# Turning row tiles one by one into shared banks at the start of a hybrid decoder block

## The chip, the cores and the metric

The kernel runs on one core of one Trainium2 chip. The metric is the device time of one execution in microseconds (us); less is better. Engines are named as the profile names them: PE is TensorE's matmul, PEld its weight load, DVE is VectorE, ACT is ScalarE, POOL is GpSimd and SP is SyncE, whose queue issues the loads and stores. "Bank" always means a PSUM bank; the kernel uses eight (a pool of six, `bank`, and one of two, `bank2`), each as a tile of 128 partitions by 512 float32.

## The reference

The block takes `x` of 512 rows by 1024 columns in float32, with one layer:

```python
h = rmsnorm(x, norm1_g)
z = h @ w_in + b_in                      # 1024 -> 6656 columns
z_glu, z_rx, z_rg, z_ga, z_gb = split(z) # two token mixers and their gates
y_a = conformer_convolution(z_glu)       # gated, 31 taps, layer norm, product
y_b = rg_lru(z_rx, z_rg)                 # 4 taps, gates per head, recurrence, product
m = sigmoid(z_ga) * y_a + sigmoid(z_gb) * y_b
x = x + m @ w_mix_out
h = rmsnorm(x, norm2_g)
x = x + (silu(h @ w1) * (h @ w3)) @ w2
return rmsnorm(x, norm_f_g)
```

Only the first two lines matter here: the first norm, and the beginning of the product with `w_in`.

## The kernel before

`x` lies in four row tiles of 128 rows, each in two halves of 512 columns (`xt[t][h]`). PE contracts over the partitions, so the normed rows have to be turned: channels must lie on the partitions. There are eight groups of 128 channels, in the text "channels 0 to 7", and each has a tile pair `h1{c}h` and `h1{c}l` of 128 channels by 512 rows. Every operand of a product is held as a high part (a copy in PE's `float32r`) and a low part (what the copy left off), and a product is three: high with high, low of the rows with high of the weights, high of the rows with low of the weights (`mm3`, L469).

The opening works on two pairs of row tiles, 0 and 1, then 2 and 3; a pair gives one half (256 columns) of every `h1` tile.

- `norm1_rows(t)` (L530) norms one row tile. ACT sums the squares of each half (L494, L500) and takes the root (L501); DVE adds the epsilon (L495), takes the reciprocal (L502) and scales both halves in place (L534).
- `rows_turned(0, n_first)` (L458) turns the first parameter rows, among them the gain `norm1_g`, on PE and copies them to `par` on DVE (L463).
- `turn_half` (L511) takes channel after channel: two transposes on PE, one from each row tile of the pair, into a tile of its own (L518); then ACT makes the high part, scaled by the gain (L521), and DVE the low part from the same tile and the high part (L522).
- A weight chunk is one column block of `w_in`, 512 KB. `emit_chunk` (L143) takes the next one in a fixed list: it issues the load on SP (L152), casts the high part on ACT and subtracts for the low part (`split_to`, L123, with rows L125 and L121), on POOL for the chunks of `w_in`. `emit_to(n)` goes on until n chunks are emitted. Loads go into four rotating buffers.
- `early_mm(i, hf)` (L541) is one of four early products, with the first four chunks, on half `hf` of the rows: 24 products of 256 columns. For the first half the eight products with the weights' low part stand last (`lo_last`).

Inside `tc.manual_schedule` (L550) PE, ACT, DVE and SP issue in the order in which the code is written; POOL's order, and everything behind the block, comes from a planner. Each engine runs its own list in order, and waits on semaphores for the others. The library that puts in those semaphores sees to it that no two engines use one bank at the same time, readers among themselves included. Loads on SP use eight semaphores in rotation: a load waits until the eighth load before it has landed.

Of the kernel before, what the change touches and what calls it, by code (L numbers as in the profile page):

```python
# [8 lines left out]
F32 = mybir.dt.float32  # L9
F32R = mybir.dt.float32r  # L10
AF = mybir.ActivationFunctionType
ALU = mybir.AluOpType

P = 128
# [12 lines left out]
ND = D // P  # L27
# [61 lines left out]
def tile_block(ctx, tc, a, out):  # L89
    nc = tc.nc  # L90
# [14 lines left out]
    def pairt(name, dtype=F32R):  # L105

        return longt(f"{name}h", dtype), longt(f"{name}l", dtype)

    def bank(name):
        return psum.tile([P, T], F32, tag="mm", name=name)  # L110

    def bank2(name):
        return psum2.tile([P, T], F32, tag="cv", name=name)

    vec, act, pe, pool_e = nc.vector, nc.scalar, nc.tensor, nc.gpsimd


    newest = {}
# [4 lines left out]
    def split_to(h, l, full, eng, copy=act.copy):  # L123

        copy(h, full)  # L125
        last = sub(eng, l, full, h.bitcast(F32))
        if eng is pool_e:
            newest["sub"] = last.ins
        return h, l
# [6 lines left out]
    chunks = []  # L136
    held = {}
    emitted = [0]

    def wchunk(key, src, kt, cols, where="hl", lo=pool_e, after=None):  # L140
        chunks.append((key, src, kt, cols, where, lo, after))

    def emit_chunk():  # L143
        key, src, kt, cols, where, lo, after = chunks[emitted[0]]
        emitted[0] += 1
        n = kt * cols
        raw = raws.tile([P, 1024], F32, tag="raw", name=f"raw_{key}")
        rv = raw[:, :n]
        if callable(src):
            src(raw)  # L150
        else:
            newest["load"] = newest["any"] = nc.sync.dma_start(rv.rearrange("p (k n) -> p k n", k=kt), src).ins  # L152
        if where == "hl":
            hl = hls.tile([P, 2, 1024], F32R, tag="hl", name=f"hl_{key}")
            h, l = split_to(hl[:, 0, :n], hl[:, 1, :n], rv, lo)
            if after:
                after(rv, h)
            held[key] = (h.rearrange("p (k n) -> p k n", k=kt), l.rearrange("p (k n) -> p k n", k=kt))
        else:
            held[key] = [  # L160
                split_to(longt(f"{key}h{i}", F32R), longt(f"{key}l{i}", F32R), rv[:, i * T : (i + 1) * T], lo)
                for i in range(2)
            ]

    def emit_to(n):
        while emitted[0] < min(len(chunks), n):
            emit_chunk()
# [6 lines left out]
    w_in = a["w_in"][0].rearrange("(k p) n -> p k n", p=P)  # L174

    def w_in_chunk(m):
        wchunk(f"in{m}", w_in[:, :, m * P : (m + 1) * P], ND, P)

    GLU, RX, RG, GA, GB = 0, 16, 26, 36, 44
    pieces = gate_pieces()  # L180
# [32 lines left out]
    for kind, j in ORDER:  # L213
        if kind == "g":
            gate_chunk(j)
        elif kind == "u":
            w_in_chunk(GLU + j)
            w_in_chunk(GLU + 8 + j)
        elif kind != "r":
            w_in_chunk({"rx": RX, "rg": RG, "gb": GB, "ga": GA}[kind] + j)  # L220
# [187 lines left out]
    n_first = ROWS[0][1] + ROWS[1][1]  # L408
    par = consts.tile([P, n_rows], F32, name="par")
    row_at = lambda c: (0, c) if c < n_first else (1 + (c - n_first) // P, (c - n_first) % P)  # L410
    at, col, parts = 0, {}, []
    for name, n in ROWS:
        col[name] = at
        src = a[name]
        src = src.rearrange("l k (c p) -> (l k c) p", p=P) if len(src.shape) == 3 else src.rearrange("l (c p) -> (l c) p", p=P)
        done = 0
        while done < n:
            m = min(n - done, P - row_at(at + done)[1])
# [5 lines left out]
    def load_rows(i):  # L424
        lo, m, src = parts[i]
        b, r = row_at(lo)
        nc.sync.dma_start(rowt[b][r : r + m, :P], src)  # L427

    x_nat = a["x"].rearrange("b (t p) d -> p (b t) d", p=P)
    xt = [[longt(f"x{t}{h}") for h in range(2)] for t in range(NT)]  # L430

    def load_x(t):
        for h in range(2):
            nc.sync.dma_start(xt[t][h], x_nat[:, t, h * T : (h + 1) * T])  # L434
# [5 lines left out]
    ident = consts.tile([P, P], F32, name="ident")  # L440
# [17 lines left out]
    def rows_turned(c0, c1):  # L458
        pt = bank2(f"par_ps{c0}")
        for c in range(c0, c1, P):  # L460
            m = min(P, c1 - c)
            pe.transpose(pt[:, c - c0 : c - c0 + m], rowt[row_at(c)[0]][:m, :P], ident[:m, :m])
        vec.tensor_copy(par[:, c0:c1], pt[:, : c1 - c0])  # L463

    def pc(name, i):
        return par[:, col[name] + i : col[name] + i + 1]


    def mm3(ps, ws, xs, lo_last=False):  # L469


        n = 3 * len(ws)
        i = 0
        three = [((wh, xh), (wh, xl), (wl, xh)) for (wh, wl), (xh, xl) in zip(ws, xs)]
        if lo_last:
            three = [q[:2] for q in three] + [q[2:] for q in three]
        for l, r in (q for qs in three for q in qs):
            pe.matmul(ps, l, r, start=i == 0, stop=i == n - 1)  # L478
            i += 1

    def w_tiles(key, kt, ahead=AHEAD):
        h, l = weights(key, ahead)
        return [(h[:, k, :], l[:, k, :]) for k in range(kt)]
# [21 lines left out]
    def rstd_of(halves, junk, between=None):  # L505
        begun = rstd_begin(halves[0], junk[0])
        if between:
            between()
        return rstd_end(begun, halves[1], junk[1])

    def turn_half(name, rows, gname, dest, hf, bk, some=range(ND)):  # L511

        cs = slice(hf * 256, hf * 256 + 256)
        for c in some:
            ps = bk[c % len(bk)](f"{name}{hf}{c}")
            for t in range(2):
                src = rows[2 * hf + t][c // 4][:, (c % 4) * P : (c % 4 + 1) * P]
                pe.transpose(ps[:, t * P : (t + 1) * P], src, ident)  # L518
            g = pc(gname, c)
            h, l = (v[:, cs] for v in dest[c])  # L520
            act.activation(h, ps[:, :256], AF.Copy, scale=g)  # L521
            last = vec.scalar_tensor_tensor(out=l, in0=ps[:, :256], scalar=g, in1=h.bitcast(F32), op0=ALU.mult, op1=ALU.subtract)  # L522
        return last.ins

    def parts_of(pair_tiles, cs=slice(0, T)):
        return [(h[:, cs], l[:, cs]) for h, l in pair_tiles]

    h1p = [pairt(f"h1{c}") for c in range(ND)]

    def norm1_rows(t):  # L530
        junk = [shortt(f"n1j{t}{h}") for h in range(2)]
        r = rstd_of(xt[t], junk)
        for h in range(2):
            vec.tensor_scalar(out=xt[t][h], in0=xt[t][h], scalar1=r, scalar2=None, op0=ALU.mult)  # L534

    HALVES = [slice(0, 256), slice(256, 512)]
    EARLY = 2
# [3 lines left out]
    def early_mm(i, hf):  # L541
        m = EARLY_IN[i]
        if hf == 0:
            early.append((m, w_tiles(f"in{m}", ND, 0), bank(f"z{m}")))
        _, ws, ps = early[i]
        mm3(ps[:, HALVES[hf]], ws, parts_of(h1p, HALVES[hf]), lo_last=hf == 0)


    ET = mybir.EngineType
    with tc.manual_schedule(engines={ET.PE, ET.Activation, ET.DVE, ET.SP}):  # L550
        norm1_rows(0)
        norm1_rows(1)
        rows_turned(0, n_first)
        emit_to(1)
        turn_half("tx", xt, "norm1_g", h1p, 0, [bank, bank, bank, bank2])
        emit_to(2)
        load_x(2)
        load_x(3)
        norm1_rows(2)
        norm1_rows(3)  # L560
        emit_to(3)
        for i in range(len(parts)):
            if i not in first:
                load_rows(i)
        early_mm(0, 0)
        early_mm(1, 0)
        turn_half("tx", xt, "norm1_g", h1p, 1, [bank2, bank, bank])
        emit_to(4)
        early_mm(2, 0)
        early_mm(3, 0)  # L570
        rows_turned(n_first, n_rows)
        for i in range(4):
            early_mm(i, 1)
    h1 = parts_of(h1p)


# [252 lines left out]
    for j in range(8):  # L829
        ws = w_tiles(f"lo{j}_0", 5) + w_tiles(f"lo{j}_1", 5)  # L830
        ps = bank(f"yb{j}")
# [113 lines left out]
    for n, j in enumerate(mixq.order()):  # L945
        ws = w_tiles(f"co{j}", ND)
        ps = bank(f"ya{j}")
# [17 lines left out]
    xs = []  # L965
# [75 lines left out]
    for hf in range(2):  # L1041
        if hf:
            turned = turn_half("th", xs, "norm2_g", h2p, 1, [bank2])
        for i in range(EARLY):
            for w_, p_ in zip(wf[i], pf[i]):
                mm3(p_[:, HALVES[hf]], w_, parts_of(h2p, HALVES[hf]))
# [189 lines left out]
```

## Time and profile before

| | before |
|---|---|
| median of three runs | 808.01 us (807.91 to 810.77) |
| the profiled execution | 808.5 us, its span 806.6 us |
| PE busy in the span | 795.6 us (99%) |
| DVE, ACT, POOL busy | 660.2, 455.4, 254.3 us |
| mean granted clock of PE | 0.996 |

The span is what the profile covers, and the time of the execution holds some 1.9 us around it. In a timeline row the first number is the start from the span's beginning in us, the second the duration, then the engine, the line of the code, the operation, the tile written and the tiles read. A note in brackets gives the time for which the engine was idle before the row, and what it waited for. `x2` means that the row merges two instructions. In a table by stretches a row gives the busy time of each engine in that stretch, then the clock that was granted to PE (1.00 is full), the share of the DMA engines and GB/s.

### The profile page before, as it was taken

How to read it: one execution, taken by the hardware profiler on the slowest of the kernel's cores; microseconds unless marked ns; L12 is line 12 of the kernel's file. 1: busy time of each engine (PE TensorE's matmuls, PEld its weight loads, DVE VectorE, ACT ScalarE, POOL GpSimd, SP SyncE). 2: the span in 40 equal slices, each digit the busy share in tenths (PEclk: the TensorE clock that was granted, in tenths of full speed). 3: DMA queues.
4: the chain of work that ended last, by engine and by line, in shares of the span. 5: the costliest groups of instructions: out<-in, count | busy, mean ns of one | idle time of the engine just before them, and what ended most of it. 6: DMA issues, size and time to landing. Idle time of an engine off the chain costs nothing.

```text
span 806.6 us, 11905 instructions
## 1 busy us (share of the span) xinstructions
PE 795.6 (99%) x4182; PEld 687.4 (85%) x4182; DVE 660.2 (82%) x1054; ACT 455.4 (56%) x643; POOL 254.3 (32%) x204
## 2 busy tenths in 40 slices
PE   8999999999999999999999999999999999999996
PEld 7988888888888888888888898999999888888885
DVE  4699899998999998786798869888887954688456
ACT  7546687776589655653336454455555432476443
POOL 3575768766777684231310042000000000000000
PEclk9999999999999999999999999999999999999999
DMA  7746476666667743578978537698889885586552
GB/s 215 191 123 172 134 200 184 181 200 186 192 185 211 228 142 108 190 228 273 298 263 271 152 94 232 195 303 263 262 260 282 241 259 183 163 268 203 177 169 105
DMA packets 207952, 165.02 MB, mean 205 GB/s; under 512 B 13096, under 2 KB 183508, under 8 KB 207892
## 3 DMA queue, kind: packets, MB, share of 16 engines
q1 hardware_dynamic: 207891, 164.26, 67.0%
q8 instruction: 33, 0.54, 0.3%
q14 instruction: 28, 0.22, 0.1%
HBM read 130.80 MB, written 30.41 MB: 200 GB/s over the span
## 4 chain that ended last, share of the span: by engine, by line
PE 96%; DMA 1%; SPq 1%; DVE 0%; POOL 0%; ACT 0%; issue 0%
PE z L478 34%; PE fr L1086 15%; PE f L478 14%; PE or L892 13%; PE yb L478 7%; PE ya L478 5%; PE mxr L892 5%; PE g L764 3%; DMA raw_in<-in_w_in_dram 1%; SPq L434 1%; PE th L518 0%; SPq L427 0%; POOL hl_in L121 0%; DVE of L1159 0%; ACT hl_in L125 0%
## 5 line engine op out<-in xcount | busy, mean ns | idle before, releaser
L637 DVE SCALAR_TENSOR_TENSOR cv<-u,par,cv 128x511 f32<-128x511 f32 (+17 forms) x240 | 162.8, 729 | 1.1 <-ACT cv L634 0.9
L121 POOL TENSOR_TENSOR hl_in<-raw_in,hl_in 128x1024 fp32r<-128x1024 f32 x52 | 125.4, 2415 | 80.9 <-ACT hl_in L125 78.7
L121 POOL TENSOR_TENSOR fws<-fws 128x256 f32<-128x256 f32 x72 | 60.7, 845 | 35.9 <-DMA fws<-in_ffn_w_dram 32.7
L125 ACT CAST hl_in<-raw_in 128x1024 fp32r<-128x1024 f32 x52 | 54.2, 1042 | 5.7 <-PE z L478 3.0
L121 DVE TENSOR_TENSOR hl_ob<-raw_ob,hl_ob 128x1024 fp32r<-128x1024 f32 (+1 forms) x23 | 27.1, 1177 | 27.4 <-ACT hl_ob L125 27.4
L125 ACT CAST hl_ob<-raw_ob 128x1024 fp32r<-128x1024 f32 (+1 forms) x23 | 23.4, 1016 | 41.1 <-PE or L892 17.3
L478 PE MATMUL z<-h10h,hl_in 128*128 128x512 f32 (+1 forms) x112 | 42.2, 379 | 0.2 <-POOL hl_in L121 0.2
L478 PE MATMUL z<-h14h,hl_in 128*128 128x512 f32 (+1 forms) x112 | 41.7, 374 | 0.0
L478 PE MATMUL z<-h12h,hl_in 128*128 128x512 f32 (+1 forms) x112 | 41.7, 374 | 0.0
L478 PE MATMUL z<-h16h,hl_in 128*128 128x512 f32 (+1 forms) x112 | 41.7, 374 | 0.0
L478 PE MATMUL z<-h11h,hl_in 128*128 128x512 f32 (+1 forms) x112 | 41.7, 374 | 0.0
L478 PE MATMUL z<-h15h,hl_in 128*128 128x512 f32 (+1 forms) x112 | 41.7, 374 | 0.0
L478 PE MATMUL z<-h17h,hl_in 128*128 128x512 f32 (+1 forms) x112 | 41.7, 374 | 0.0
L478 PE MATMUL z<-h13h,hl_in 128*128 128x512 f32 (+1 forms) x112 | 41.7, 374 | 0.0
L125 ACT CAST hl_f<-raw_f 128x1024 fp32r<-128x1024 f32 x20 | 20.9, 1050 | 34.2 <-PE f L478 19.6
L1086 PE MATMUL fr<-hs_0h,hl_ft 128*128 128x256 f32 x192 | 35.5, 283 | 0.0
L121 DVE TENSOR_TENSOR hl_f<-raw_f,hl_f 128x1024 fp32r<-128x1024 f32 x20 | 26.7, 1337 | 10.3 <-ACT hl_f L125 10.3
L121 DVE TENSOR_TENSOR hl_fb<-raw_fb,hl_fb 128x1024 fp32r<-128x1024 f32 x18 | 23.1, 1282 | 13.4 <-ACT hl_fb L125 13.3
L125 ACT CAST hl_ft<-raw_ft 128x1024 fp32r<-128x1024 f32 x24 | 25.1, 1048 | 12.9 <-issue 9.5
L121 DVE TENSOR_TENSOR hl_ft<-raw_ft,hl_ft 128x1024 fp32r<-128x1024 f32 x24 | 29.1, 1217 | 3.7 <-ACT hl_ft L125 3.7
L1086 PEld LDWEIGHTS fr<-hs_0h,hl_ft 128*128 128x128 f32 x192 | 30.4, 192 | 0.0
L125 ACT CAST hl_fb<-raw_fb 128x1024 fp32r<-128x1024 f32 x18 | 18.9, 1050 | 18.5 <-PE fr L1086 7.1
(906 smaller groups left out, 2610.0 us busy)
## 6 DMA issues: line engine op xcount, KB each, us to landing
raw_in<-in_w_in_dram SPq DMA_DIRECT2D x52, 512.0 KB
fws<-in_ffn_w_dram SPq DMA_DIRECT2D x48, 256.0 KB
fs<-fws SPq DMA_DIRECT2D x24, 512.0 KB
raw_ft<-fs SPq DMA_DIRECT2D x24, 512.0 KB
fwso<-in_ffn_w_dram SPq DMA_DIRECT2D x44, 256.0 KB
ot<-fwso SPq DMA_DIRECT2D x22, 512.0 KB
raw_f<-in_ffn_w_dram SPq DMA_DIRECT2D x20, 512.0 KB
raw_fb<-in_ffn_w_dram SPq DMA_DIRECT2D x36, 256.0 KB
```

What stands on the lines that cost most here:

```text
L121: return eng.tensor_tensor(out=o, in0=x, in1=y, op=ALU.subtract)
L125: copy(h, full)
L434: nc.sync.dma_start(xt[t][h], x_nat[:, t, h * T : (h + 1) * T])
L478: pe.matmul(ps, l, r, start=i == 0, stop=i == n - 1)
L637: vec.scalar_tensor_tensor(out=acc[c][:, s:], in0=u[c][:, : T - s], scalar=dw(c, s), in1=acc[c][:, s:], op0=ALU.mult, op1=ALU.add)
L764: pe.matmul(ps, l, r, start=k == 0, stop=k == len(mms) - 1)
L892: pe.matmul(banks[i], l_[:, ts], r_, start=start and n == 0, stop=stop and n == 2, skip_group_check=again)
L1086: pe.matmul(ps[:, HALVES[i]], lw[:, 4 * i + c, :], rx_, start=not (again or i or c or m), stop=bool(i and c == 3 and m == 2), skip_group_c ...
```

## The change

Four things are changed, all in the opening block.

1. Row tiles are turned one by one. `turn_rows(t, ps)` turns all eight channels of one row tile; `ps` are four banks, a quarter of the channels in each: channels 2q and 2q+1 share bank q, each with 256 columns, of which a row tile fills 128. When both tiles of a pair are turned, `turned_parts` makes the high and low parts of the eight channels on ACT and DVE in the order of the channels.
2. The first product of the first half takes its 24 products in an order written out: high and low rows of channels 0 to 4, then the products with the weights' low part in between those of channels 5 to 7.
3. The loads of the third and the fourth chunk are issued right behind those of row tiles 2 and 3 (`load_chunk`), which for the fourth is ahead of the thirteen loads of the other parameter rows.
4. The low part of the second chunk goes to DVE instead of POOL, and the order of the calls changes: the small turn of parameters stands between the two scalings of tile 1, and the first two early products stand between the norm of tile 2 and that of tile 3.

```diff
+    def load_chunk(i):
+        key, src, kt, cols = chunks[i][:4]
         raw = raws.tile([P, 1024], F32, tag="raw", name=f"raw_{key}")
...
+        loaded_raw[i] = raw
+
+    def emit_chunk():
+        key, src, kt, cols, where, lo, after = chunks[emitted[0]]
+        if emitted[0] not in loaded_raw:
+            load_chunk(emitted[0])
+        raw = loaded_raw.pop(emitted[0])
+        emitted[0] += 1
...
-        wchunk(f"in{m}", w_in[:, :, m * P : (m + 1) * P], ND, P)
+        wchunk(f"in{m}", w_in[:, :, m * P : (m + 1) * P], ND, P, lo=pool_e if len(chunks) != 1 else vec)
...
+    def turn_rows(t, ps):
+
+        for c in range(ND):
+            at = 256 * (c % 2) + P * (t % 2)
+            pe.transpose(ps[c // 2][:, at : at + P], xt[t][c // 4][:, (c % 4) * P : (c % 4 + 1) * P], ident)
+
+    def turned_parts(hf, ps):
+        cs = slice(hf * 256, hf * 256 + 256)
+        for c in range(ND):
+            g, at = pc("norm1_g", c), 256 * (c % 2)
+            p_ = ps[c // 2][:, at : at + 256]
+            h, l = (v[:, cs] for v in h1p[c])
+            act.activation(h, p_, AF.Copy, scale=g)
+            vec.scalar_tensor_tensor(out=l, in0=p_, scalar=g, in1=h.bitcast(F32), op0=ALU.mult, op1=ALU.subtract)
...
+        if (i, hf) == (0, 0):
+
+            order = [(m, c) for c in range(5) for m in (0, 1)]
+            order += [(2, 0), (2, 1), (0, 5), (1, 5), (2, 2), (2, 3), (0, 6), (1, 6), (2, 4), (2, 5), (0, 7), (2, 6), (2, 7), (1, 7)]
+            xs = parts_of(h1p, HALVES[0])
+            for n, (m, c) in enumerate(order):
+                (wh, wl), (xh, xl) = ws[c], xs[c]
+                l, r = ((wh, xh), (wh, xl), (wl, xh))[m]
+                pe.matmul(ps[:, HALVES[0]], l, r, start=n == 0, stop=n == len(order) - 1)
+            return
...
+        turned = [bank(f"tx0{q}") for q in range(4)]
         norm1_rows(0)
-        norm1_rows(1)
-        rows_turned(0, n_first)
+        turn_rows(0, turned)
+        norm1_rows(1, lambda: rows_turned(0, n_first))
         emit_to(1)
-        turn_half("tx", xt, "norm1_g", h1p, 0, [bank, bank, bank, bank2])
+        turn_rows(1, turned)
+        turned_parts(0, turned)
         emit_to(2)
         load_x(2)
         load_x(3)
+        load_chunk(2)
+        load_chunk(3)
         norm1_rows(2)
+        early_mm(0, 0)
+        early_mm(1, 0)
+        turned = [(bank2, bank)[q // 2](f"tx1{q}") for q in range(4)]
+        turn_rows(2, turned)
         norm1_rows(3)
         emit_to(3)
         for i in range(len(parts)):
             if i not in first:
                 load_rows(i)
-        early_mm(0, 0)
-        early_mm(1, 0)
-        turn_half("tx", xt, "norm1_g", h1p, 1, [bank2, bank, bank])
+        turn_rows(3, turned)
+        turned_parts(1, turned)
         emit_to(4)
         early_mm(2, 0)
         early_mm(3, 0)
```

More of the change, by code (lines that the diff above doesn't have):

```diff
@@ L138, in tile_block @@
     emitted = [0]
+    loaded_raw = {}
     def wchunk(key, src, kt, cols, where="hl", lo=pool_e, after=None):
         chunks.append((key, src, kt, cols, where, lo, after))
[L143 to L146, printed above, removed]
+    def load_chunk(i):
+        key, src, kt, cols = chunks[i][:4]
         raw = raws.tile([P, 1024], F32, tag="raw", name=f"raw_{key}")
-        rv = raw[:, :n]
         if callable(src):
@@ L151, in emit_chunk @@
         else:
-            newest["load"] = newest["any"] = nc.sync.dma_start(rv.rearrange("p (k n) -> p k n", k=kt), src).ins
+            newest["load"] = newest["any"] = nc.sync.dma_start(raw[:, : kt * cols].rearrange("p (k n) -> p k n", k=kt), src).ins
+        loaded_raw[i] = raw
[5 more added lines that the diff above has]
+        emitted[0] += 1
+        n = kt * cols
+        rv = raw[:, :n]
         if where == "hl":
@@ L528, in tile_block, with norm1_rows @@
     h1p = [pairt(f"h1{c}") for c in range(ND)]
-    def norm1_rows(t):
+    def norm1_rows(t, between=lambda: None):
         junk = [shortt(f"n1j{t}{h}") for h in range(2)]
@@ L534, in norm1_rows @@
             vec.tensor_scalar(out=xt[t][h], in0=xt[t][h], scalar1=r, scalar2=None, op0=ALU.mult)
+            if h == 0:
+                between()
     HALVES = [slice(0, 256), slice(256, 512)]
```

## The prediction

> **What bounds the kernel now.** I read the engine totals and the chain that ended last first, then the busy time of every engine by stage, and last the timeline of the stage that the change touches.
>
> ```profile
> PE 795.6 (99%) x4182; PEld 687.4 (85%) x4182; DVE 660.2 (82%) x1054; ACT 455.4 (56%) x643; POOL 254.3 (32%) x204
> PE 96%; DMA 1%; SPq 1%; DVE 0%; POOL 0%; ACT 0%; issue 0%
> ```
>
> ```profile
> 8.00:12.10 4.10, 3.42 (x17) 3.20 (x17) 2.89 (x9) 3.43 (x8) 2.04 (x1) 0.58 1.08 348
> ...
> 28.00:50.00 22.00, 22.00 (x141) 20.05 (x140) 19.98 (x45) 10.76 (x14) 13.09 (x8) 1.00 0.58 158
> 50.00:100.00 50.00, 50.00 (x222) 41.37 (x221) 47.33 (x74) 28.31 (x38) 32.21 (x26) 1.00 0.50 138
> 100.00:400.00 300.00, 300.00 (x1323) 248.33 (x1322) 270.18 (x392) 196.96 (x252) 177.54 (x148) 1.00 0.67 199
> 400.00:700.00 300.00, 299.65 (x1902) 272.92 (x1901) 237.84 (x414) 144.18 (x217) 18.93 (x14) 1.00 0.73 228
> ```
>
> TensorE is the bound. In the table by stage (stretch, its length, then busy time of PE, PEld, DVE, ACT and POOL, then the granted clock), PE is busy in every microsecond from 28 to 400 and misses 0.35 us up to 700. So whatever the opening moves in the time at which PE gets past its early products, the end moves by the same amount. After the opening block both programs hold the same instructions in the same order on every engine. The question is when PE starts on the second halves of the four early products: 27.05 us now.
>
> The path to that point, in the timeline of before (start, duration, engine, line, operation):
>
> ```profile
> 8.94 1.05 ACT L125 CAST hl_in<-raw_in 128x1024 fp32r<-128x1024 f32 x1 [0.67 <-DMA raw_in<-in_w_in_dram]
> 9.89 0.47 ACT L521 ACTIVATE h10h<-tx,par 128x256 fp32r<-128x256 f32 x1
> 10.06 2.37 POOL L121 TENSOR_TENSOR hl_in<-raw_in,hl_in 128x1024 fp32r<-128x1024 f32 x1 [8.76 <-ACT hl_in L125]
> 10.26 0.46 ACT L521 ACTIVATE h11h<-tx,par 128x256 fp32r<-128x256 f32 x1
> 10.39 0.48 DVE L522 SCALAR_TENSOR_TENSOR h10l<-tx,par,h10h 128x256 fp32r<-128x256 f32 x1 [0.88 <-ACT h10h L521]
> 10.79 0.47 DVE L522 SCALAR_TENSOR_TENSOR h11l<-tx,par,h11h 128x256 fp32r<-128x256 f32 x1
> 12.13 0.36 PE L478 MATMUL z<-h10h,hl_in 128*128 128x256 f32 x1
> 12.48 0.47 ACT L521 ACTIVATE h17h<-tx,par 128x256 fp32r<-128x256 f32 x1
> 12.84 1.04 ACT L125 CAST hl_in<-raw_in 128x1024 fp32r<-128x1024 f32 x1
> 13.14 0.47 DVE L522 SCALAR_TENSOR_TENSOR h17l<-tx,par,h17h 128x256 fp32r<-128x256 f32 x1
> 13.96 2.41 POOL L121 TENSOR_TENSOR hl_in<-raw_in,hl_in 128x1024 fp32r<-128x1024 f32 x1 [1.53 <-ACT hl_in L125]
> 14.54 0.16 DVE L495 TENSOR_SCALAR stats<-stats 128x1 f32<-128x1 f32 x1 [0.93 <-ACT n1j L494]
> 15.09 0.28 PE L478 MATMUL z<-h10h,hl_in 128*128 128x256 f32 x1
> 15.15 0.30 ACT L501 ACTIVATE stats<-stats 128x1 f32<-128x1 f32 x1
> 15.68 1.37 DVE L534 TENSOR_SCALAR x<-x,stats 128x512 f32<-128x512 f32 x2
> 17.20 0.29 ACT L501 ACTIVATE stats<-stats 128x1 f32<-128x1 f32 x1 [0.53 <-DVE stats L495]
> 17.41 1.03 ACT L125 CAST hl_in<-raw_in 128x1024 fp32r<-128x1024 f32 x1
> 17.73 0.88 DVE L534 TENSOR_SCALAR x<-x,stats 128x512 f32<-128x512 f32 x2
> 17.97 2.54 PE L518 MATMUL tx<-ident,x 128*128 128x128 f32 x16
> 18.64 0.48 ACT L521 ACTIVATE h10h<-tx,par 128x256 fp32r<-128x256 f32 x1 [0.20 <-PE tx L518]
> 21.15 0.52 ACT L521 ACTIVATE h17h<-tx,par 128x256 fp32r<-128x256 f32 x1
> 22.18 1.05 ACT L125 CAST hl_in<-raw_in 128x1024 fp32r<-128x1024 f32 x1 [0.51 <-DMA raw_in<-in_w_in_dram]
> 23.30 4.74 POOL L121 TENSOR_TENSOR hl_in<-raw_in,hl_in 128x1024 fp32r<-128x1024 f32 x2 [2.42 <-ACT hl_in L125]
> 25.75 0.39 PE L478 MATMUL z<-h10h,hl_in 128*128 128x256 f32 x1 [0.23 <-POOL hl_in L121]
> 27.05 0.37 PE L478 MATMUL z<-h10h,hl_in 128*128 128x256 f32 x1
> ```
>
> The last wait before 27.05 is not PE's own: the fourth early product waits for the low part of the fourth chunk (POOL; the row holds two of 2.37), that for its cast (22.18), and the cast stands on ScalarE behind the eight high parts of the second pair of tiles, begun at 18.64. That chain through ScalarE sets the sum.
>
> **The change part by part.**
>
> *Shared banks.* Before, each of the eight channels had a tile of its own: h11h began at 10.26 while VectorE's h10l, begun at 10.39, read another bank. Now channels 2q and 2q+1 share a bank, and the built program has a new wait: in each half h11h, h13h, h15h and h17h wait for the count that VectorE's h10l, h12l, h14l and h16l set. Nothing of before shows that wait, so its price comes from hand-overs. ScalarE to VectorE: 10.39 − 9.89 = 0.50. VectorE to ScalarE: 0.48 for the part and the gap of this pair,
>
> ```profile
> 51.18 0.74 DVE L721 SCALAR_TENSOR_TENSOR xb<-z,par,xb 128x509 f32<-128x509 f32 x1
> ...
> 52.01 0.62 ACT L125 CAST xb0h<-xb 128x512 fp32r<-128x512 f32 x1 [1.59 <-DVE xb L721]
> ```
>
> 52.01 − 51.92 = 0.09, so 0.57. Two low parts in a row on VectorE: 10.79 − 10.39 = 0.40. Two channels take 0.50 + 0.57 + 0.40 = 1.47 us, where ScalarE took (12.48 − 9.89) / 7 x 2 = 0.74. From the start of h10h to that of h17h: 0.50 + 0.57 + 3 x 1.47 = 5.48 instead of 2.59, **2.89 us more in each half**. The lower end takes the gap of 0.03 that stands between h10h's end (10.36) and h10l: some 0.25 less. Below nothing only if the wait did not hold ScalarE, and it stands in the program.
>
> *First half.* h10h stays at 9.89: it follows the first cast, which waits for its load. The transposes of tile 0 start earlier, and the small parameter turn and its copy now stand between: the copy delays the scaling of x11 by some 0.2, covered as h14h isn't due before 12.8. h17h starts at 15.37, h17l ends near 16.35. The new order of the first product lets PE follow each part, so it ends at 16.5 instead of 15.09: the order is worth nothing, since PE waits for parts.
>
> *Second chunk.* Its cast moves from 12.84 to 15.37 + 0.36 = 15.73 and ends at 16.77. Its low part now goes to VectorE for about
>
> ```profile
> L121 DVE TENSOR_TENSOR hl_ob<-raw_ob,hl_ob 128x1024 fp32r<-128x1024 f32 (+1 forms) x23 | 27.1, 1177 | 27.4 <-ACT hl_ob L125 27.4
> ```
>
> 1.18 us, until 17.95, where POOL would take 2.41. The second product runs from 16.8 to 19.7 without a wait. But behind that low part on VectorE stands the statistic of tile 2: 14.54 becomes 17.95. From there the spacings of before: ScalarE's root at 18.2 (17.95 + 0.16 + 0.09), the scaling 0.53 later at 18.73; it takes 0.88 instead of 1.37 if POOL, idle then, is what stretched it (an estimate from the two L534 rows; else 0.49 more). Statistic of tile 3 at 19.6, its root 0.23 later, scaling of tile 3 at 20.35 where it was 17.73. PE has turned tile 2 by 21.0 (19.7 + 8 x 2.54/16), when tile 3's first half is scaled (20.8): at most 0.2 more. The four tiles of the second pair lie in two banks of the second pool and two that the first pair left, free since 16.4: nothing.
>
> *Second half.* h10h came 0.91 after that scaling's start; now it needs two channels of tile 3 instead of one, 0.11 more: 21.37. h17h starts at 26.85, the fourth cast 0.37 later at 27.2 (was 22.18), its low part 1.12 later at 28.3, until 30.7; PE at 30.75 where it was 25.75: **5.0 us later**. With the short gaps 4.5, with the slow scaling 5.5.
>
> *The two loads moved up.* On SP the fourth chunk's load passes thirteen loads of parameter rows, ahead of which only the third's issue stands as before. It removes the 0.51 that the cast at 22.18 waited for its load; by 27.2 either place would do: nothing. The rows come up to one 512 KB load later; PE needs them only behind the fourth product.
>
> *The clock.* PE now stands idle between the third product (after the transposes, 21.8 to 24.7) and the fourth's first part at 28.25: 3.5 us. What idling costs shows at the start, where PE did little from 6 to 8.7:
>
> ```profile
> 6.00:7.00 1.00, 0.02 (x1) 0.00 (x0) 0.78 (x3) 0.81 (x3) 0.00 (x0) 1.00 1.11 324
> 7.00:8.00 1.00, 0.15 (x1) 0.13 (x1) 0.33 (x2) 0.82 (x4) 0.00 (x0) 1.00 1.08 259
> ...
> 8.50:9.00 0.50, 0.00 (x0) 0.00 (x0) 0.50 (x2) 0.07 (x1) 0.00 (x0) 0.70 1.21 300
> ...
> 12.00:12.50 0.50, 0.50 (x6) 0.50 (x5) 0.50 (x3) 0.50 (x3) 0.43 (x1) 0.89 1.11 340
> ```
>
> The granted clock is 0.5 from 8.7 to 12.1 (0.70 and 0.89 are means over half microseconds), 3.4 us that follow a lull of some 2.7. The same after the new lull would run the fourth product at half speed: at most 3.4 / 2 = 1.7, less the 0.6 that its high parts wait for the low one: 1.1. The ends are 0 and 1.7; I take 1.0, as the new lull is longer than the one in the rows. The Trainium skill, "TensorE: Matmul & The Clock Gate", section "What's actually happening", says that the clock falls to half after an idle window of about 3.4 us that runs free of the kernel; the trace agrees with its length, and by that rule it depends on where the window falls, 0 or about 1.1.
>
> The sum: 5.0 + 1.0 = 6.0 us on the profiled execution's 808.5 (its span of 806.6 and 1.9 around it), 814.5. That execution lies 0.5 above the median of the runs, 808.01, so I predict 814.0.
>
> **The rivals.**
>
> *The parts don't take turns* (faster). If ScalarE and VectorE ran on beside each other, the first product would end near 13.9, the second, with its low part by VectorE at 15.1, near 17.0, and the fourth cast would start right behind h17h and not wait for its load. Second parts would begin at 18.2 (tile 3's scaling gains 0.3 from an idle POOL), the cast at 21.2, POOL would end at 24.7, PE at 24.75: 1.0 us sooner, 807.0. It decides only if the four waits are met before ScalarE comes to them; by the rows h10l starts 0.13 after h11h used to. The Trainium skill, "PSUM — Partial Sum Buffer", section "PSUM bank collisions raise a hardware error", forbids two engines in one bank at once, two readers included; no run here shows a collision, but by that rule the wait can't be left out. Chance 0.03.
>
> *No clock loss.* The lull falls across two windows, each half busy: 5.0 alone, 813.0, from 812.5 to 813.5. Chance 0.27.
>
> *Two clock losses.* While PE is paced by the parts (10.4 to 16.4) it does 24 products of (15.09 − 12.13) / 24 = 0.12 at full clock, half of the time. If the clock falls behind that too, the second product, 2.9 us, takes up to 1.0 more, of which 0.9 reaches the second half's h10h, since PE has then not turned tile 2 when tile 3 is scaled: 814.9. Chance 0.25.
>
> *Less than the turns cost.* Something of the chain through tile 2 is hidden: the delay of one half alone, 2.9, gives 810.9. Chance 0.10.
>
> **How the numbers follow.** My case, the turns and one clock loss, has 0.35. Half a per cent, 4.04 us, is about what a measurement of this kernel can tell from no change: the line lies at 812.05. Slower by more: my case, the two losses and most of the case without, 0.35 + 0.25 + 0.22 = 0.82, less 0.04 for a time around the kernel that differs by half a microsecond: 0.78. Faster by over 0.5% would need 4 us, more than PE waits in the whole opening: 0.01. Within: 0.21. The range goes from 811.6 (short gaps, no clock loss, 0.9 of spread in the runs) to 816.0 (slow scaling, both losses); left out are the first and the fourth rival and the tails, 0.2.
>
> **What would show it.** Right: ScalarE's idle time at its part line ends on VectorE, with eight such waits of about 0.65 each; h17h starts 5.4 to 5.5 us after h10h in both halves; the fourth cast starts near 27; PE's second halves begin near 32 or 33; the clock shows 0.5 in a second stretch before 33. Wrong: parts at 0.37 us spacing, a fourth cast before 24, or a PE that has idle time behind 35 us in which the delay is taken back.

## The result, and the profile after

| | before | after |
|---|---|---|
| median of six runs each | 809.21 us (807.91 to 810.77) | 814.99 us (813.87 to 816.29) |
| the profiled execution | 808.5 us, span 806.6 | 816.29 us, span 814.2 |
| PE busy | 795.6 us | 799.8 us |
| PE starts on the second halves | 27.05 us | 34.63 us |

The changed kernel takes 1.0069 of the time before, 95% interval 1.0051 to 1.0087: 5.8 us more, where the prediction had 6.0. Three more runs of before had moved its median from 808.01 to 809.21. The profiled execution of after is the longest of its six, so its rows show more than the 5.8 of the medians.

The engine totals and the chain that ended last, of after:

```profile
PE 799.8 (98%) x4182; PEld 690.6 (85%) x4182; DVE 662.7 (81%) x1055; ACT 455.7 (56%) x643; POOL 252.7 (31%) x203
PE 96%; DVE 1%; DMA 1%; ACT 1%; SPq 0%; issue 0%
```

Two rows of the table by stage of after (stretch, length, busy time of PE, PEld, DVE, ACT, POOL, then clock, DMA share, GB/s):

```profile
100.00:400.00 300.00, 300.00 (x1323) 248.11 (x1323) 271.20 (x392) 199.31 (x255) 180.34 (x149) 1.00 0.65 193
400.00:700.00 300.00, 299.65 (x1902) 272.85 (x1901) 238.63 (x410) 142.68 (x215) 21.61 (x16) 1.00 0.74 231
```

PE is busy in these as before, to the hundredth: 300.00 and 299.65. Nothing of the delay is taken back behind the opening; all 7.6 us by which this span is longer lie ahead of the second halves (34.63 against 27.05). The opening, in the timeline of after:

```profile
9.85 1.04 ACT L125 CAST hl_in<-raw_in 128x1024 fp32r<-128x1024 f32 x1 [2.30 <-DMA raw_in<-in_w_in_dram]
10.80 0.47 ACT L545 ACTIVATE h10h<-tx,par 128x256 fp32r<-128x256 f32 x1
11.30 0.48 DVE L546 SCALAR_TENSOR_TENSOR h10l<-tx,par,h10h 128x256 fp32r<-128x256 f32 x1 [2.51 <-ACT h10h L545]
11.82 0.48 ACT L545 ACTIVATE h11h<-tx,par 128x256 fp32r<-128x256 f32 x1 [0.55 <-DVE h10l L546]
12.19 0.47 ACT L545 ACTIVATE h12h<-tx,par 128x256 fp32r<-128x256 f32 x1
13.24 0.48 ACT L545 ACTIVATE h13h<-tx,par 128x256 fp32r<-128x256 f32 x1 [0.58 <-DVE h12l L546]
16.08 0.47 ACT L545 ACTIVATE h17h<-tx,par 128x256 fp32r<-128x256 f32 x1 [0.58 <-DVE h16l L546]
16.45 1.03 ACT L125 CAST hl_in<-raw_in 128x1024 fp32r<-128x1024 f32 x1
18.66 0.14 DVE L503 TENSOR_SCALAR stats<-stats 128x1 f32<-128x1 f32 x1
19.42 0.88 DVE L557 TENSOR_SCALAR x<-x,stats 128x512 f32<-128x512 f32 x2
20.99 0.88 DVE L557 TENSOR_SCALAR x<-x,stats 128x512 f32<-128x512 f32 x2
23.17 0.47 ACT L545 ACTIVATE h10h<-tx,par 128x256 fp32r<-128x256 f32 x1 [1.47 <-PE tx L537]
28.45 0.47 ACT L545 ACTIVATE h17h<-tx,par 128x256 fp32r<-128x256 f32 x1 [0.58 <-DVE h16l L546]
28.82 1.98 ACT L125 CAST hl_in<-raw_in 128x1024 fp32r<-128x1024 f32 x2
29.91 0.39 PE L486 MATMUL z<-h10h,hl_in 128*128 128x256 f32 x1 [3.25 <-ACT hl_in L125]
34.38 0.48 PE L470 MATMUL par_ps<-ident,rows 128*128 128x128 f32 x3
34.63 0.37 PE L486 MATMUL z<-h10h,hl_in 128*128 128x256 f32 x1
```

What to see: the second channel of each bank waits for VectorE's low part of the first (11.82, 13.24, 16.08), so two channels take 13.24 − 11.82 = 1.42 us. From h10h to h17h it is 5.28 in both halves (16.08 − 10.80, 28.45 − 23.17), where it was 2.59 and 2.51. The fourth cast, the first of the two in the row of 28.82, stands right behind the last high part, and when the fourth product starts at 29.91, PE has been idle for 3.25 us. What ended ScalarE's idle time at its part line, in the waits of after (us, times):

```profile
  PE tx L537: 1.5, 1
  DVE h14l L546: 1.2, 2
  DVE h12l L546: 1.2, 2
  DVE h16l L546: 1.2, 2
  DVE h10l L546: 1.1, 2
```

Eight waits on VectorE, 4.7 us, and one on PE of 1.47.

**A measure that leaves out when the first load lands.** In the profiles the first cast, which waits for the load of the first chunk, starts anywhere from 8.32 to 9.85 us, in kernels that issue that load alike. Why is open. So I count from the first cast to four places: the second half's h10h, the fourth cast, and the turn of the large parameter rows (L462, L470), which stands on PE between the first and the second halves. From there to the end of the span it is 779.7 to 781.0 us in the profiles of this study, so differences of a few tenths in the turn say little about the time.

| us behind the first cast | second h10h | fourth cast | parameter turn |
|---|---|---|---|
| before | 9.70 | 13.24 | 17.86 |
| after | 13.32 | 18.97 | 24.53 |
| after, once more | 12.20 | 17.85 | 24.23 |

By this measure the change costs 24.53 − 17.86 = 6.67 us in the profile, and the other 0.9 of the 7.6 is the late first cast.

### The profile page after: what moved, and what is told of

Its sections match the earlier page's. It is cut to its first block, busy times and chain, and to the rows that moved or that the text cites. A ratio compares the mean times of both kernels' runs of the same rounds, so it can differ in the third digit from the quotient of the medians.

```text
span 814.2 us, 11909 instructions
## 1 busy us (share of the span) xinstructions
PE 799.8 (98%) x4182; PEld 690.6 (85%) x4182; DVE 662.7 (81%) x1055; ACT 455.7 (56%) x643; POOL 252.7 (31%) x203
## 4 chain that ended last, share of the span: by engine, by line
PE 96%; DVE 1%; DMA 1%; ACT 1%; SPq 0%; issue 0%
PE z L486 35%; PE fr L1129 15%; PE f L486 14%; PE or L935 13%; PE yb L486 7%; PE ya L486 5%; PE mxr L935 5%; PE g L807 3%; DMA raw_in<-in_w_in_dram 1%; PE z L579 1%; PE th L526 0%; DVE of L1202 0%; SPq L442 0%; PE tx L537 0%; DVE h10l L546 0%
## 5 line engine op out<-in xcount | busy, mean ns | idle before, releaser
L121 POOL TENSOR_TENSOR hl_in<-raw_in,hl_in 128x1024 fp32r<-128x1024 f32 x51 | 123.0, 2415 | 90.8 <-ACT hl_in L125 85.4
```

The source lines that it names most:

```text
L121: return eng.tensor_tensor(out=o, in0=x, in1=y, op=ALU.subtract)
```

## The experiments

The theory: with two neighbouring channels in a bank ScalarE and VectorE take turns, this reaches PE through the fourth cast, and PE's clock falls on top. The rivals: another part of the change makes the delay (the order of the calls, the loads, the low part on VectorE), or the turns are hidden and the clock alone costs. Medians are against runs of before on the same chip.

| kernel | edit | median, before beside it | ratio (95%) | parameter turn |
|---|---|---|---|---|
| four_apart | after, channels c and c+4 share a bank | 808.64, 809.05 | 0.9996 (0.9986 to 1.0006) | 18.55 |
| pairs_only | before, neighbours share a bank | 816.10, 809.05 | 1.0088 (1.0073 to 1.0103) | 25.18 |
| first_half_apart | after, c and c+4 in the first half only | 812.51, 809.05 | 1.0042 (1.0029 to 1.0055) | 20.70 |
| lull_filled | after, idle products in the second lull | 813.69, 809.05 | 1.0056 (1.0041 to 1.0071) | 22.99 |
| after once more | none | 815.50, 809.03 | 1.0072 (1.0060 to 1.0085) | 24.23 |
| both_lulls_filled | after, idle products in both lulls | 814.20, 809.03 | 1.0064 (1.0052 to 1.0076) | 22.43 |
| cast_ahead | after, fourth cast ahead of the second parts | 810.08, 809.03 | 1.0011 (1.0002 to 1.0020) | 19.25 |
| apart_cast_ahead | four_apart and cast_ahead | 807.45, 809.03 | 0.9980 (0.9971 to 0.9989) | 15.85 |
| low_on_pool | after, second low part on POOL | 816.38 (one run), 809.16 | | 24.55 |
| before_cast_ahead | before, loads up and fourth cast ahead | 808.96, 809.16 | 0.9996 (0.9987 to 1.0004) | 18.02 |

The changed kernel once more, beside the second group of runs:

> The changed kernel as it is, beside the three below on one chip, as their measure. All theories: 5 to 6.5 us above before.

Measured: 815.50, 6.5 us over before, with eight waits of 0.55 to 0.58 again.

### Who shares a bank

```diff
-            at = 256 * (c % 2) + P * (t % 2)
-            pe.transpose(ps[c // 2][:, at : at + P], xt[t][c // 4][:, (c % 4) * P : (c % 4 + 1) * P], ident)
+            at = 256 * (c // 4) + P * (t % 2)
+            pe.transpose(ps[c % 4][:, at : at + P], xt[t][c // 4][:, (c % 4) * P : (c % 4 + 1) * P], ident)
...
-            g, at = pc("norm1_g", c), 256 * (c % 2)
-            p_ = ps[c // 2][:, at : at + 256]
+            g, at = pc("norm1_g", c), 256 * (c // 4)
+            p_ = ps[c % 4][:, at : at + 256]
```

> The changed kernel with one edit: channels c and c+4 share a bank instead of 2q and 2q+1, in both halves; the order of the parts stays. Theory (the turns that two channels of one bank force on ScalarE and VectorE make the change slower): h14h to h17h now wait for low parts that were done long ago, parts follow each other at 0.37 us, h17h starts 2.6 us after h10h in both halves, the fourth cast starts near 21 to 22, no second lull of PE, and the time is that of before, between 1 us less and 0.5 us more. Rival (the moved order, the low part on VectorE or the moved loads cost the time): 4 to 6 us above before, as the changed kernel.

Measured: 0.4 us below before, which is no difference by its interval, where after loses 5.8. Timeline of four_apart:

```profile
9.82 0.47 ACT L545 ACTIVATE h10h<-tx,par 128x256 fp32r<-128x256 f32 x1
12.32 0.52 ACT L545 ACTIVATE h17h<-tx,par 128x256 fp32r<-128x256 f32 x1
22.75 1.09 ACT L125 CAST hl_in<-raw_in 128x1024 fp32r<-128x1024 f32 x1
23.89 0.39 PE L486 MATMUL z<-h10h,hl_in 128*128 128x256 f32 x1 [0.85 <-ACT hl_in L125]
27.42 0.48 PE L470 MATMUL par_ps<-ident,rows 128*128 128x128 f32 x3
```

The parts run at (12.32 − 9.82) / 7 = 0.36 us again, and PE's idle time before the fourth product falls from 3.25 to 0.85. The banks are still shared, by two; four channels lie between the sharers. The fourth cast, at 22.75, is a little later than expected, and by the trace the parameter turn comes 0.69 later than in before (18.55 against 17.86). A stretch of slow clock is in it, with no turns: the clock is 0.50 from 11.33 to 14.74, and the second product starts 15.38 − 8.87 = 6.51 us behind the first cast, where that of first_half_apart below, with the same first half at full clock, starts 14.76 − 9.31 = 5.45 behind. The medians do not show this loss. The order also seems to have a small price: in the second half it is 19.88 − 18.26 = 1.62 us from PE's first transpose to h10h, in after 23.17 − 21.88 = 1.29, which fits that the bank of h10h now takes channel 4 as well before it may be read.

The opposite, in before: the neighbours share a bank and nothing else changes.

```diff
+            if name == "tx":
+                if c % 2 == 0:
+                    two = bk[c // 2 % len(bk)](f"{name}{hf}{c}")
+                    for c_ in (c, c + 1):
+                        for t in range(2):
...
+                            at_ = 256 * (c_ - c) + t * P
+                            pe.transpose(two[:, at_ : at_ + P], src, ident)
+                ps = two[:, 256 * (c % 2) : 256 * (c % 2) + 256]
```

> The kernel before with one edit: its turning of the first norm puts two neighbouring channels into one bank (both are turned, then their parts are made); nothing else of the change. Theory: the shared banks alone cost nearly all of it, h17h starts 5.3 us after h10h in both halves, and the time is 4.5 to 7 us above before. Rival (shared banks are cheap, the rest of the change costs): within 1 us of before.

```profile
15.08 0.47 ACT L531 ACTIVATE h17h<-tx,par 128x256 fp32r<-128x256 f32 x1 [0.58 <-DVE h16l L532]
28.22 0.47 ACT L531 ACTIVATE h17h<-tx,par 128x256 fp32r<-128x256 f32 x1 [0.58 <-DVE h16l L532]
```

Measured: 7.05 us slower, just above the range expected. In these rows of pairs_only the last high part waits for VectorE as in after, and h10h to h17h is again 5.28 in both halves (9.80 to 15.08, 22.94 to 28.22). The one edit makes the whole loss, and some more; that the rest of the change gives about 1 us back is what the medians say, but the two intervals overlap.

One half only:

```diff
-            at = 256 * (c % 2) + P * (t % 2)
+            b_, p2 = (c % 4, c // 4) if t < 2 else (c // 2, c % 2)
+            at = 256 * p2 + P * (t % 2)
...
-            g, at = pc("norm1_g", c), 256 * (c % 2)
+            b_, p2 = (c % 4, c // 4) if hf == 0 else (c // 2, c % 2)
```

> The changed kernel with channels c and c+4 sharing a bank in the first half alone; the second half keeps neighbours in one bank. Theory (each half costs 2.7 us of turns, and the first also the clock loss of 1.0 to 1.2 that the paced first product brings): 3.7 to 3.9 us below the changed kernel, 1.9 to 2.2 above before, with one cold stretch near 27 to 31 us. Rival (the halves hide in each other, so that one half's turns alone cost nearly all): 4 us or more above before.

Measured: 3.46, more than expected. The second h10h comes 9.62 behind the first cast, as in before; the fourth cast 5.66 behind h10h instead of 3.54; and from cast to parameter turn it is 5.42 instead of 4.62, as the clock falls to half from 27.08 to 30.49. So by the trace the second half's turns cost 2.0 us by themselves, and the clock 0.8, together 2.8 of the 3.46. The expectation had halved the loss of after without leaving the second stretch of slow clock whole.

### The clock

The products added here write a bank that nothing reads.

```diff
+    def fill(n, b_=bank2):
+        fp = b_("fill")
+        (wh, _), (xh, _) = early[0][1][0], h1p[0]
+        for _ in range(n):
+            pe.matmul(fp[:, :256], wh, xh[:, :256], start=True, stop=True)
...
         early_mm(2, 0)
+        fill(26)
         early_mm(3, 0)
```

> The changed kernel with 26 products of 256 columns into a spare bank, whose result nothing reads, put between the third and the fourth early product, where PE stands idle for 3.4 us. Theory (the lull halves the clock for the fourth product): the granted clock stays at 1.00 from 20 us on, the fourth product takes about 3.4 instead of 4.5 us, and the time is 1.1 us below the changed kernel, 4.7 above before. Rival (the clock falls for another reason, or the fourth product waits for its low part anyway): as the changed kernel, 5.8 above before, or 0.3 more for fillers that come late.

Measured: 4.64. The fourth product ran at full clock, from cast to parameter turn 4.63 us, as in before (4.62). In both_lulls_filled, 14 small products stand ahead of the first product as well, and two more behind each of its first ten:

```diff
         turn_rows(1, turned)
+        fill(14)
...
+                if n < 10:
+                    for _ in range(2):
+                        pe.matmul(fp[:, :256], ws[0][0], xs[0][0], start=True, stop=True)
...
         early_mm(2, 0)
+        fill(26, (early[0][1][0][0], h1p[0][0][:, :256]))
```

> The changed kernel with idle products into a spare bank at three places: 14 small ones before the first product, two behind each of its first ten products, and the 26 between the third and the fourth. Theory (the slow stretch that follows the paced first product delays the turning of tile 2 and so the second half's parts): the granted clock is 1.00 from 12 us on, the second half's h10h follows the first half's by 11.2 instead of 12.4 us, and the time is 2.3 us below the changed kernel. Rival (the first product is paced by its parts, so its clock is worth nothing): 1.1 us below it, as with the second lull filled alone; fillers in the way of products would show as PE busy while a part is ready.

```profile
8.84 1.05 ACT L125 CAST hl_in<-raw_in 128x1024 fp32r<-128x1024 f32 x1 [1.54 <-DMA raw_in<-in_w_in_dram]
20.99 0.47 ACT L545 ACTIVATE h10h<-tx,par 128x256 fp32r<-128x256 f32 x1 [0.31 <-PE tx L537]
26.65 1.99 ACT L125 CAST hl_in<-raw_in 128x1024 fp32r<-128x1024 f32 x2
31.27 0.48 PE L470 MATMUL par_ps<-ident,rows 128*128 128x128 f32 x3
```

This is the timeline of both_lulls_filled. Its clock is 1.00 throughout the opening, and the parameter turn comes 31.27 − 8.84 = 22.43 behind the first cast: the turns alone cost 22.43 − 17.86 = 4.57 us, and 2.1 of the 6.67 are the clock. (Before has a slow stretch of its own, from 8.7 to 12.1; its second h10h waited 0.20 for PE, so up to there that can have cost it no more than this.) In the runs the two versions of after differ by 1.3 us only, where 2.3 were expected, and their intervals overlap, so for the 2.1 the trace alone speaks. Nor do the runs show that filling the first lull gains anything over filling the second alone: both_lulls_filled is 5.2 over the before beside it, lull_filled 4.6.

### Through which step it reaches PE

```diff
         turn_rows(3, turned)
-        turned_parts(1, turned)
         emit_to(4)
+        turned_parts(1, turned)
         early_mm(2, 0)
```

> The changed kernel with one call moved: the cast of the fourth chunk stands ahead of the second half's parts on ScalarE instead of behind them; the shared banks stay. Theory (the second half's turns reach PE through the fourth cast alone): the fourth product follows the third without a wait, no second lull and no second slow stretch, and the time is 4 to 5 us below the changed kernel although the parts still follow each other at 1.4 us a pair. Rival (PE then waits for the parts themselves, in the second halves of the products): 2 us below it or less, with PE idle on the part lines behind 29 us.

Measured: 1.05 us over before, 5.4 less than the changed kernel beside it. Timeline of cast_ahead:

```profile
19.14 1.98 ACT L125 CAST hl_in<-raw_in 128x1024 fp32r<-128x1024 f32 x2
21.36 0.47 ACT L545 ACTIVATE h10h<-tx,par 128x256 fp32r<-128x256 f32 x1 [0.24 <-PE tx L537]
26.63 0.47 ACT L545 ACTIVATE h17h<-tx,par 128x256 fp32r<-128x256 f32 x1 [0.58 <-DVE h16l L546]
27.57 0.48 PE L470 MATMUL par_ps<-ident,rows 128*128 128x128 f32 x3
```

The turns are all there (26.63 − 21.36 = 5.27), but with the fourth cast done by 21.1 they hold nobody up: PE runs from 12 to 32 us without idle time, and the second lull with its slow clock is gone. So in this profile the second half's turns reach the end through the fourth cast, and only through it. The 1.39 by which the parameter turn is still behind that of before (19.25 against 17.86) lie ahead of that: the first half's turns stay, and the clock is 0.50 from 11.00 to 17.83.

Both mends together:

> Channels c and c+4 in a bank, in both halves, and the fourth cast ahead of the second half's parts. Theory (that cast and its low part are the last waits of PE in the opening, 0.85 and 0.28 us when only the banks are apart, and the casts are what held the fourth product): the fourth product follows the third at once, and the time is 1.2 to 1.8 us below before. Rival (the time is then held by something else in the opening, such as the parts that now start a cast later): within 0.5 us of before.

```profile
17.82 1.98 ACT L125 CAST hl_in<-raw_in 128x1024 fp32r<-128x1024 f32 x2
19.70 0.47 ACT L545 ACTIVATE h10h<-tx,par 128x256 fp32r<-128x256 f32 x1
25.57 0.48 PE L470 MATMUL par_ps<-ident,rows 128*128 128x128 f32 x3
```

Measured: 807.45, 1.6 us less than before, and faster than both kernels. Its clock is 1.00 from 10 to 35 us. Does before need the shared banks for that, or only the earlier cast?

```diff
         load_x(3)
+        load_chunk(2)
+        load_chunk(3)
...
-        turn_half("tx", xt, "norm1_g", h1p, 1, [bank2, bank, bank])
         emit_to(4)
+        turn_half("tx", xt, "norm1_g", h1p, 1, [bank2, bank, bank])
```

> The kernel before (a bank per channel) with two things of the others: the two loads moved up and the fourth cast ahead of the second half's parts. Theory (with a bank per channel the transposes wait for parts to free their banks, so parts that start a cast later hold PE's transposes and the third product): 0.3 us above before, between 0.3 below and 0.8 above, with PE idle among the transposes for 1 us or more. Rival (the order of the cast and the parts is all that made the version with channels c and c+4 in a bank faster): 1.2 to 1.8 us below before, as that one.

Measured: no gain, 0.2 below before. The edit takes `load_chunk` over from the change. PE's transposes in before_cast_ahead, where each channel has a bank of its own:

```profile
18.87 1.42 PE L526 MATMUL tx<-ident,x 128*128 128x128 f32 x11 [0.25 <-DVE x L542]
20.93 0.83 PE L526 MATMUL tx<-ident,x 128*128 128x128 f32 x4 [0.64 <-DVE h10l L530]
```

With the cast ahead the parts come later, and PE has to wait 0.64 us for the low part of the first channel (h10l), whose bank the seventh, with the last four transposes, takes over. In apart_cast_ahead, with four banks for eight channels, PE does not wait among its transposes. So the sharing of banks can pay, in another order of the channels than the change gave it, and with the cast ahead. How much of the gain is the banks' is not shown: PE waits 0.25 + 0.64 = 0.89 us here, while the parameter turns of the two kernels lie 18.02 − 15.85 = 2.17 apart, and they also differ in the turning of tiles one by one, the order of the first product and the low part on VectorE.

### The second low part

```diff
-        wchunk(f"in{m}", w_in[:, :, m * P : (m + 1) * P], ND, P, lo=pool_e if len(chunks) != 1 else vec)
+        wchunk(f"in{m}", w_in[:, :, m * P : (m + 1) * P], ND, P, lo=pool_e)
```

> The changed kernel with the low part of the second chunk on GpSimd again. Theory (its move to VectorE delays the statistic of tile 2, but ScalarE's sums stand there by themselves until nearly the same time): from the first cast's start to the second half's h10h as in the changed kernel, within 0.4 us, as an earlier statistic is met by a slower scaling beside GpSimd's subtraction (1.37 instead of 0.88 us). Rival (that move costs what the prediction's step gave it): 0.5 us or more sooner, or, if the second product then waits for its low part, later by the same.

```profile
16.55 2.40 POOL L121 TENSOR_TENSOR hl_in<-raw_in,hl_in 128x1024 fp32r<-128x1024 f32 x1 [4.22 <-ACT hl_in L125]
17.13 0.15 DVE L503 TENSOR_SCALAR stats<-stats 128x1 f32<-128x1 f32 x1 [1.07 <-ACT n1j L502]
18.26 1.37 DVE L557 TENSOR_SCALAR x<-x,stats 128x512 f32<-128x512 f32 x2
20.32 0.88 DVE L557 TENSOR_SCALAR x<-x,stats 128x512 f32<-128x512 f32 x2
```

In low_on_pool the first cast is at 8.84. Counted from it, the second h10h comes at 21.36 − 8.84 = 12.52: 0.80 sooner than in after, and 0.32 later than in after once more, so the 0.4 expected holds against one execution of after and not against the other. The steps decide more: the statistic of tile 2 comes at 8.29 (after: 8.81), but its scaling takes 1.37 us beside POOL's subtraction instead of the 0.88 of after, where POOL is idle, and tile 3 is scaled at 11.48, in both executions of after at 11.14. The parameter turn is the same as in the first of them, 24.55 and 24.53, but that one has a slow stretch more ahead of its second h10h. After once more has the same slow stretches as low_on_pool, one in the first lull and two in the second, and there the difference reaches the turn: 24.55 against 24.23.

## Why the prediction was right

The time, 814.99, lies 1.0 over the 814.0 predicted and inside the range, and slower had 0.78. The difference, 5.8, is 0.2 under the 6.0 predicted; the 1.0 comes from before, whose median rose by 1.2 with three more runs. By the steps, behind the first cast, as differences to before:

| step | predicted | after | both_lulls_filled (no slow clock) |
|---|---|---|---|
| up to the second half's h10h | 2.73 | 3.62 | 2.45 |
| from there to the fourth cast | 2.29 | 2.11 | 2.12 |
| from there to the parameter turn | 1.0 | 0.94 | 0.00 |
| sum | 6.0 | 6.67 | 4.57 |

- *Shared banks*: right. The 5.48 predicted from h10h to h17h are 5.28. The term that was too long is the hand-over from VectorE to ScalarE: 11.82 − 11.30 = 0.52 instead of 0.57, four times in a half; the waits are 0.55 to 0.58 each, where I had about 0.65. pairs_only shows that it is this edit, four_apart that the rest of the change, taken together, costs no measurable amount; its parts could still cancel.
- *First half*: h10h stands 0.95 behind the first cast, as before. That the new order of the first product is worth nothing stays open, as no run changes it alone. That the product ends at 16.5, 6.6 behind h10h, held at full clock only: in both_lulls_filled the second one starts 16.52 − 9.79 = 6.73 behind h10h, in after 18.22 − 10.80 = 7.42.
- *Second chunk*: the sum right, its reason wrong in part. I put the late statistic of tile 2 down to the low part on VectorE ahead of it. low_on_pool has no such low part there, and its statistic comes only 0.52 earlier: it waits for ScalarE's sum of squares, and that stands behind the same turns. Of the 0.52 only 0.15 reaches the scaling (9.42 behind the first cast, in after 9.57), as on ScalarE the sum of the second half stands ahead of the root too. The estimate that POOL stretches the scaling held: 1.37 beside it, 0.88 without. Taken together the move to VectorE is no delay but makes tile 3's scaling 0.49 − 0.15 = 0.34 sooner.
- *Second half*: right, the path and the size. cast_ahead cuts the path at the step named and takes 5.4 us away.
- *Two loads moved up*: the third and the fourth cast of after wait for no load. The fourth had waited 0.51; either place would have done, as predicted: pairs_only loads in the old order, and its fourth cast, at 28.59, waits for no load either.
- *The clock*: the term that was mis-sized. For the second lull the 1.0 held in the first execution of after (0.94); in the second it was 6.38 − 4.62 = 1.76, above the 1.7 that I had as its upper end, since the clock stayed low for two stretches. What my own case left out, and the rival of two clock losses had, is the first lull: in after the clock is 0.5 from 13.18 to 20.01 as well, the second product runs at 0.21 us per product there (18.43 − 18.22) instead of 0.12, PE turns tile 2 late, and ScalarE's second h10h waits 1.47 for it. That is 13.32 − 12.15 = 1.17 us against the 0.9 of the rival, but in the second execution it is 12.20 − 12.15 = 0.05. So by the traces the clock takes 2.1 and 1.8 us, where my case had 1.0 and the rival, at a chance of 0.25, 1.9: the rival has the sum, and its mechanism in one execution of two. By the medians the 6.0 is nearer to the 5.8 than the rival's 6.9, and its 814.9 lies on the time only because before's median rose. The sum without the clock was 0.4 too high, which hid part of the missing clock. That the difference came out within 0.2 is luck in part.
- *The range*: its upper end does not follow from its terms. The slow scaling and both losses give 808.01 + 5.5 + 1.9 = 815.4; the other 0.6 of 816.0 has no term.
- *What was not foreseen*: the second halves start at 34.63, not near 32 or 33. 0.9 of this is the first load's late landing in that execution, which no step held; the rest is mostly the slow clock in the first lull.
- *The parts don't take turns*: fell with the eight waits. That four_apart runs at 0.36 spacing with the same banks shows the rival's mechanism where the order permits it. The Trainium skill, "PSUM — Partial Sum Buffer", section "PSUM bank collisions raise a hardware error", has engines kept apart by bank, also two readers; the waits of after agree with that, 0.55 to 0.58 each, and no run here shows a collision.

Open stays why the first load lands at different times, and the 1.0 or so that pairs_only loses beyond after; 0.32 of that fits the second chunk's low part on POOL, as pairs_only scales tile 3 at 20.31 − 8.85 = 11.46 behind the first cast, close to the 11.48 of low_on_pool.

## What to carry to other kernels

When two engines read the same bank one after the other, put the sharers far apart in the order of the parts: neighbours in a bank made two engines that had worked side by side take turns (1.42 us for two channels instead of 0.72), and partners four apart did not. Then look at what stands behind the slowed work on its in-order engine: here a cast which PE waited for, and moving that one call ahead was worth 5.4 us with the slow parts left as they were. Here shared banks went with a gain only where such an order and the earlier cast stood together (807.45 us against 809.03 before); the order alone gave no gain that the runs show, and the cast alone left 1.05.

## What was not expected of the hardware

The slow clock comes in stretches of 3.41 us, one or two in a row, and in the second lull the number goes with where the lull falls. PE alone in such stretches of after (stretch, length, busy time, clock, DMA share, GB/s):

```profile
13.18:16.59 3.41, 3.41 (x14) 0.50 0.94 229
16.59:20.01 3.42, 3.42 (x18) 0.50 0.07 17
...
26.83:30.25 3.42, 0.34 (x3) 1.00 0.13 36
30.25:33.66 3.41, 3.41 (x19) 0.50 0.04 12
```

and of after, once more:

```profile
13.63:17.04 3.41, 3.27 (x15) 0.50 0.84 214
23.87:27.28 3.41, 1.27 (x11) 1.00 1.04 264
27.28:30.69 3.41, 2.30 (x10) 0.50 0.02 6
30.69:34.11 3.42, 3.42 (x18) 0.50 0.52 153
```

The lull is 3.25 us in both. In the first execution it fills one stretch almost whole, PE starts 0.34 ahead of the next and has the full clock back after one. In the second execution it is cut in two: the stretch with 1.27 us of work lowers the clock, the next, with 2.30 of 3.41, doesn't raise it, and PE has it back only after a third: 24.23 − 17.85 = 6.38 us from the fourth cast to the parameter turn instead of 5.56. The Trainium skill, "TensorE: Matmul & The Clock Gate", section "What's actually happening", has a window of 3413 ns that runs free, and one busy window that gives the clock back. The length agrees, 3.41; and the stretch with 2.30 of 3.41, 67% by the records, was not busy enough. In the first lull the difference is the other way, two stretches in the first execution and one in the second, so that both lose about the same in all: 2.1 and 1.8 us over the 22.43 without slow clock. The busy time does not tell these two apart: 13.18 to 16.59 is busy for all of 3.41 us by the records and did not give the clock back, 13.63 to 17.04 with 3.27 did. But the records hold waiting too. In the first of these stretches products that wait for parts start 0.5 us apart (13.26, 13.77, 14.29), where the pace at half clock is 0.21, and 12 products start in it against 14 in the second. Where the line lies is open.
